# Separate semaphores for the first K halves, with re-made engine orders, in a cosine-similarity attention kernel

## The chip, the cores and the metric

The kernel runs on one NeuronCore of a Trainium2 chip. The metric is the device time of one launch in microseconds (us), as the median of several runs; lower is better. The profile pages and traces used below come from single profiled executions on that core.

## The reference

Q, K and V are f32 arrays of shape 8 x 12 x 512 x 64 (batch, head, sequence, dim), tau is 0.1. Each of the 96 heads is an independent attention over unit-length rows:

```
Q_norm = Q / (norm(Q, axis=-1) + 1e-10)
K_norm = K / (norm(K, axis=-1) + 1e-10)
scores = einsum('bhqd,bhkd->bhqk', Q_norm, K_norm) / tau
weights = exp(scores - max(scores)) ; weights = weights / (sum(weights) + 1e-10)
out = einsum('bhqk,bhkd->bhqd', weights, V)
```

## The kernel before

The 96 heads are worked as 48 pairs, numbered s = 0 to 47. A pair goes through these operations, which the program names by a tuple; this document writes the tuple with dots, so `SQ.3.0` is the tuple ("SQ", 3, 0). The middle number is the pair. For operations with w, w=0 is Q and w=1 is K; h is the head of the pair, c the 128-row chunk of the keys.

- `LD.s.w`: load of Q or K (256 KB, line 289), on the queue of SP. `LV.s`: load of V (256 KB, line 292). Pair 0 is loaded in halves of 128 KB by head, `LD.0.w.h` (line 286), the two Q halves from SP's queue and the two K halves from ACT's.
- `SQ`: squares for the norms. POOL does most of them as one 128x1024 operation per pair (line 313); pair 0 is done in halves (`SQ.0.0.h` on ACT line 227, `SQ.0.1.h` on POOL line 229), and pairs 1 and 2 are split between POOL (line 308) and ACT (line 306).
- `SSQ`: PE adds up the squares into PSUM (line 330). `RED`: DVE finishes the sum (lines 233, 337, 341).
- `LOG`, `NRMS`, `NEW`: the reciprocal root; on ACT by Ln and Exp for pairs 0 to 2 (lines 236, 240, 355, 357), by Newton steps on DVE (lines 362 to 371) for the later groups of two pairs.
- `SCL`: multiply Q or K with it, to bf16 (lines 246 and 389), Q on DVE, K mostly on POOL. `TR`: four transposes on PE (lines 254, 256, 395). `EVA`: copy out of PSUM (lines 265, 267, 402).
- `SCO.s.c`: scores on PE (line 429). `EXP.s.c`: exponential on ACT (line 445), 128x1024 each, four for a pair; the first two chunks of pair 0 are done by head, as `EXP.0.c.h`.
- `VC.s`: V to bf16 on POOL (line 450). `PV`: weights times V on PE (line 459). `RCP`, `NRM`: normalisation on DVE (lines 474, 476). `ST`: store from SP's queue (line 483).

There is no scheduler when the kernel is built: the table `ORDER` lists, for each of the five engines, the numbers of the operations in the sequence in which that engine issues them. The numbers were made ahead of time by a planner, from costs and due times. An engine issues strictly in that sequence; a wait in front of one operation holds back everything behind it, on SP's queue too. Negative numbers in the PE list are filler matmuls of so many columns (line 188), which only keep PE occupied; a `warm` of 8 matmuls of 512 columns (line 185) stands ahead of them and needs the identity matrix that POOL makes (`one`, `eye`; `vone` is a memset of the ones column of V).

Operations that a DMA performs get a semaphore by the name in `slot`; two operations with one name share one semaphore, and each adds 16. The count that a consumer waits for is handed out while the engines are walked in the sequence sp, pool, dve, pe, act:

```
dma_count[o.slot] += 16
o.sem, o.val, o.inc = dma_sems[o.slot], dma_count[o.slot], 16
```

In the kernel before, the halves of pair 0 are called `first{w}_{h}` and the loads of pairs 1 and 2 `first{s}_{w}`. `LD.0.1.0` and `LD.1.0` are thus both `first1_0`, and `LD.0.1.1` and `LD.1.1` both `first1_1`. SP is walked ahead of ACT, so pair 1's load has the value 16 and pair 0's K half the value 32: whoever wants the K half waits for both transfers.

Ring sizes that matter below: 18 buffers of Q and K, 6 of V as loaded (so `LV.s` waits for `VC.(s-6)`), 8 of the output.

Of the kernel before, what the change touches and what calls it, by code (L numbers as in the profile page):

```python
# [106 lines left out]
def bass_cosine_similarity_attention_kernel(  # L107
# [15 lines left out]
    R_QK, R_V, R_SQ, R_QN, R_QT, R_ET, R_O, R_X = 18, 6, 6, 3, 3, 3, 8, 3  # L123
# [27 lines left out]
    P = Program(nc)  # L151
# [10 lines left out]
    group, first = [], []  # L162
# [4 lines left out]
    def src(x, s):  # L167
        b, h = divmod(2 * s, NHEAD)
        return x[b, h : h + 2].rearrange("h (p t) d -> p h (t d)", t=NT)

    def key(name, s, *rest):
        return (name, s) + rest if s >= 0 else None
# [102 lines left out]
    def pair(s):  # L275
# [6 lines left out]
        for w, x in ((0, Q), (1, K)):  # L282
            if s == 0:
                for h in range(2):
                    P.add(("LD", 0, w, h), "act" if w else "sp", "ldh", -1000 + h,  [],
                          lambda e, w=w, x=x, h=h: e.dma_start(out=qk[iq][:, w, h], in_=src(x, s)[:, h]), slot=f"first{w}_{h}")  # L286
                continue
            P.add(("LD", s, w), "sp", "ld", s, [*([("SCL", 0, w, 0), ("SCL", 0, w, 1), ("SQ", 0, w, 0), ("SQ", 0, w, 1)] if s == R_QK else [key("SCL", s - R_QK, w), key("SQ", s - R_QK, w if s - R_QK in SQ_ON else 0)])],
                  lambda e, w=w, x=x: e.dma_start(out=qk[iq][:, w], in_=src(x, s)),
                  slot=f"first{s}_{w}" if s <= 2 else f"qk{iq}")  # L290
# [223 lines left out]
def slack(s, most):  # L514
# [5 lines left out]
        "7 8 64 65 103 104 143 142 187 186 11 297 221 220 66 262 415 263 296 188 264 105 338 339 144 568 63 525 222 372 "  # L520
        "373 416 340 449 796 417 450 298 526 491 492 602 374 493 102 645 644 451 567 797 831 678 527 601 185 754 830 "
        "722 720 141 756 679 950 1059 1103 721 949 261 873 908 219 755 569 646 603 680 1026 984 1060 1213 1289 874 414 "
        "1288 295 907 1178 337 832 1025 371 1255 951 798 1102 983 490 1212 600 448 1366 1136 1407 566 643 1331 1137 524 "
        "1332 909 1365 1061 875 753 1179 1518 1636 677 985 1517 1594 795 1254 1104 719 1027 1408 829 1483 1637 1138 "
        "1670 1180 1595 1333 1214 1441 1256 1290 948 1747 1442 1484 1024 1443 1561 1367 1562 872 1560 1788 906 1712 "
        "1789 982 1409 1519 1596 1746 1713 1101 1671 1485 1672 1058 1748 1177 1135 1822 1824 1287 1253 1823 1364 1440 "
        "1211 1406 1790 1638 1330 1482 1559 1714 1669 1745 1516 1635 1711 1787 1593 1821 1864 1865 "
    ),
    "pool": (
        "0 1 2 4 14 27 22 67 35 107 145 189 50 223 89 265 206 282 128 299 172 341 237 248 271 375 358 418 313 452 347 "  # L530
        "401 494 435 324 424 477 511 528 570 553 466 500 604 647 681 542 576 799 723 587 833 653 757 630 740 664 695 "
        "876 729 952 706 910 771 805 1028 986 782 859 882 816 1105 1062 1139 924 958 1181 893 1215 935 1000 1034 969 "
        "1257 1011 1122 1291 1088 1045 1111 1164 1368 1334 1153 1187 1351 1240 1444 1410 1229 1198 1317 1263 1469 1486 "
        "1393 1563 1340 1546 1520 1274 1427 1597 1382 1416 1622 1715 1673 1458 1492 1503 1580 1639 1774 1851 1569 1791 "
        "1825 1749 1611 1656 1645 1808 1698 1687 1721 1763 1797 1732 1839 "
    ),
    "dve": (
        "5 13 15 26 28 19 32 24 21 72 70 34 75 109 78 76 111 80 114 115 117 147 190 119 149 192 55 150 56 151 152 153 "
        "154 61 155 226 156 157 159 158 62 161 193 163 224 266 100 268 195 227 101 228 94 229 197 230 95 231 139 232 "
        "302 234 233 140 133 235 134 342 239 300 344 183 269 303 184 304 177 305 178 306 273 307 376 308 217 309 310 "  # L540
        "311 211 378 212 218 345 315 419 421 253 379 254 380 453 381 259 382 260 383 349 384 287 455 385 386 288 387 "
        "388 390 422 392 495 497 329 456 293 457 294 458 330 459 426 460 335 461 336 463 462 529 464 363 498 364 531 "
        "369 468 370 571 573 532 406 533 407 534 605 535 412 536 502 537 413 538 440 539 607 441 574 648 540 446 482 "
        "650 447 608 544 609 483 610 682 611 488 612 489 613 578 615 614 616 617 619 516 684 517 522 724 523 621 726 "
        "800 685 558 686 559 687 651 688 564 689 565 690 692 691 655 693 592 598 760 593 599 697 727 758 802 635 761 "
        "636 762 877 763 731 764 641 765 642 766 669 767 768 836 670 769 675 953 676 834 773 803 879 911 837 711 838 "
        "712 839 807 840 717 841 718 842 913 745 844 843 845 846 848 746 751 987 850 752 955 880 914 1029 787 915 788 "
        "916 884 917 793 918 794 919 989 920 921 922 821 956 822 1063 1106 827 926 1031 828 990 864 991 865 992 1140 "
        "993 870 994 871 995 960 996 997 1182 904 998 898 905 899 1065 1002 1032 1216 1108 940 1066 941 1067 946 1068 "
        "1069 947 1070 1258 1071 1036 1072 1073 980 1075 974 1074 981 975 1142 1077 1292 1079 1109 1184 1016 1143 1022 "  # L550
        "1144 1145 1017 1146 1023 1147 1113 1148 1150 1149 1335 1151 1056 1050 1218 1051 1057 1155 1369 1260 1185 1219 "
        "1093 1220 1094 1221 1099 1222 1100 1223 1189 1224 1294 1226 1225 1127 1227 1128 1261 1133 1134 1231 1411 1337 "
        "1445 1295 1169 1296 1170 1297 1265 1298 1175 1299 1487 1300 1203 1371 1301 1176 1302 1204 1303 1304 1306 1209 "
        "1564 1210 1308 1338 1245 1413 1372 1246 1521 1373 1251 1374 1252 1375 1342 1376 1279 1447 1377 1378 1379 1280 "
        "1380 1285 1414 1286 1384 1489 1322 1448 1449 1323 1450 1328 1451 1329 1452 1598 1453 1418 1454 1455 1456 1523 "
        "1674 1356 1357 1716 1362 1460 1490 1398 1566 1363 1524 1399 1525 1526 1527 1528 1529 1530 1494 1404 1531 1405 "
        "1432 1600 1433 1533 1532 1438 1535 1567 1537 1439 1474 1642 1640 1475 1601 1602 1603 1571 1604 1480 1605 1481 "
        "1606 1676 1608 1607 1508 1609 1509 1643 1514 1826 1515 1613 1551 1718 1677 1678 1552 1557 1750 1679 1558 1647 "
        "1680 1681 1682 1752 1585 1683 1586 1684 1792 1591 1685 1592 1689 1794 1753 1719 1754 1755 1627 1756 1628 1757 "
        "1758 1760 1759 1633 1723 1634 1661 1662 1761 1667 1668 1765 1795 1703 1828 1829 1704 1830 1799 1831 1832 1833 "  # L560
        "1709 1834 1710 1737 1835 1836 1837 1743 1738 1744 1841 1785 1786 1779 1780 1813 1814 1819 1820 1856 1857 1862 "
        "1863 "
    ),
    "pe": (
        "6 -512 -256 -256 -256 -192 23 20 -256 -256 71 69 -128 33 36 108 -128 42 38 39 110 79 43 77 46 48 148 146 81 "
        "116 118 83 51 52 53 54 191 85 57 58 87 59 60 225 120 122 160 124 96 97 90 162 126 98 99 164 267 91 166 92 93 "
        "168 194 196 135 136 170 137 138 301 198 129 130 131 132 200 179 180 202 236 238 204 181 173 182 343 240 272 "
        "174 242 175 176 270 244 213 214 246 215 216 207 274 208 209 210 377 276 312 278 314 249 250 280 251 252 420 "
        "255 316 346 256 257 318 283 284 258 348 320 285 286 454 322 289 350 352 290 325 389 354 391 326 327 356 291 "
        "328 496 292 393 425 423 395 331 332 333 334 397 359 399 360 361 365 366 362 427 530 367 368 429 465 467 431 "  # L570
        "402 403 404 433 405 572 501 469 408 409 499 471 410 411 436 437 473 438 439 606 475 442 443 503 444 445 505 "
        "478 479 480 481 649 507 543 541 509 484 485 486 545 487 577 547 575 549 518 519 512 513 514 551 520 515 683 "
        "579 521 618 581 620 554 555 583 556 557 725 585 560 561 622 654 562 624 563 588 589 590 626 652 591 594 595 "
        "628 759 596 597 656 694 696 658 631 637 632 638 660 633 634 801 662 639 640 698 728 730 700 665 666 667 668 "
        "702 835 704 671 672 673 674 732 770 734 707 708 709 772 736 710 713 878 738 806 774 804 714 715 776 716 741 "
        "742 743 778 744 912 780 747 748 749 808 750 847 810 849 783 784 812 785 786 954 814 883 789 851 881 790 853 "
# [64 lines left out]
```

## Time and profile before

| | us |
|---|---|
| median of 9 runs | 194.49 (193.02 to 196.02) |
| time of the profiled execution | 194.47 |
| span in its trace | 192.5 |
| ACT busy (L445 alone) | 182.2 (176.7) |
| PE, DVE, POOL busy | 175.2, 168.4, 155.3 |
| first exponential starts, in the span | 12.19 |

The profiled execution lies on the median of the runs to 0.02 us; 1.97 us of its time are outside the span. The page gives busy time by engine, then by group of instructions with the line of the kernel; the trace behind it gives each engine's instructions in order of time. Times in the text are from the start of the span.

### The profile page before, as it was taken

The page shows a single profiled execution, that of the slowest core. Times are in us where ns is not written, and L with a number is a line of the kernel's source. Part 1 is how long each engine was busy: PE and PEld are TensorE (multiplying, and loading weights), DVE is VectorE, ACT ScalarE, POOL GpSimd, SP SyncE. Part 2 cuts the span into 40 slices and gives each one's busy share as a digit, 9 for nine tenths or more (in the row PEclk, how much of TensorE's full clock was granted, in tenths as well). Part 3 has the DMA queues.
Part 4 walks back from the last instruction along what each step waited for, and adds up shares of the span by engine and source line. Part 5 has one row for each costly group of instructions (what it writes and reads, how often), then busy time and mean ns, then how long its engine had stood idle before and what let it go on. Part 6 is the DMA issues. An engine that isn't in the chain of part 4 may idle for free.

```text
span 192.5 us, 6756 instructions
## 1 busy us (share of the span) xinstructions
PE 175.2 (91%) x2729; PEld 110.6 (57%) x2729; DVE 168.4 (88%) x593; ACT 182.2 (95%) x211; POOL 155.3 (81%) x144
## 2 busy tenths in 40 slices
PE   7399899989999999999899999989899999999993
PEld 2266466646665566566566556656565666555552
DVE  1569999999999999999989999998999999977844
ACT  4469999999999999999999999999999999999993
POOL 2699869999998999999998999897999975524200
PEclk9789999999999999999999999999999999999999
DMA  5999999988999999999299995897692156301067
GB/s 173 356 351 348 296 339 358 361 284 248 348 357 378 337 347 373 379 380 330 100 302 377 363 367 155 251 371 256 217 313 79 56 164 221 110 4 58 0 197 242
DMA packets 52302, 50.76 MB, mean 264 GB/s; under 512 B 3120, under 2 KB 52272, under 8 KB 52272
## 3 DMA queue, kind: packets, MB, share of 16 engines
q1 hardware_dynamic: 51984, 50.08, 79.3%
q8 instruction: 21, 0.34, 0.8%
q10 hardware_dynamic: 288, 0.26, 0.4%
q14 instruction: 9, 0.07, 0.1%
HBM read 37.75 MB, written 12.58 MB: 261 GB/s over the span
## 4 chain that ended last, share of the span: by engine, by line
ACT 82%; DMA 4%; PE 4%; POOL 4%; DVE 2%; issue 1%; SPq 1%; DVEq 0%; POOLq 0%
ACT et L445 81%; DMA out_dram<-ob 2%; DMA qk<-in_Q_dram 2%; POOL sq L313 2%; PE ops L459 1%; DVE ob L476 1%; PE scps L429 1%; POOL vb L450 1%; PE ops L330 1%; POOL qn L389 1%; SPq L286 0%; DVE qn L389 0%; DVE rd L474 0%; PE scps L256 0%; POOL qn L246 0%
## 5 line engine op out<-in xcount | busy, mean ns | idle before, releaser
L445 ACT ACTIVATE et<-scps 128x1024 bf16<-128x1024 f32 (+1 forms) x195 | 176.7, 1169 | 0.3 <-PE scps L429 0.3
L313 POOL TENSOR_TENSOR sq<-qk 128x1024 bf16<-128x1024 f32 x45 | 84.6, 1893 | 1.0 <-DMA qk<-in_Q_dram 0.6
L429 PE MATMUL scps<-qt 64*128 64x512 bf16 x384 | 75.5, 386 | 9.0 <-ACT et L445 4.9
L459 PE MATMUL ops<-vb,et 128*128 128x65 bf16 x1536 | 76.5, 195 | 0.8 <-POOL vb L450 0.5
L459 PEld LDWEIGHTS ops<-vb,et 128*128 128x128 bf16 x1536 | 57.6, 98 | 29.7 <-issue 21.0
L389 POOL TENSOR_TENSOR qn<-qk,rk 128x512 bf16<-128x512 f32 x37 | 38.1, 1042 | 17.1 <-DVE rk L367 16.8
L476 DVE TENSOR_TENSOR ob<-ops,rd 128x256 f32<-128x256 f32 x96 | 39.6, 418 | 1.3 <-DMA out_dram<-ob 0.7
L389 DVE TENSOR_TENSOR qn<-qk,nps 128x512 bf16<-128x512 f32 x57 | 37.8, 677 | 0.0
L429 PEld LDWEIGHTS scps<-qt 64*128 64x128 bf16 x384 | 19.2, 92 | 28.1 <-ACT et L445 11.9
L402 DVE COPY qt<-tps 128x1024 bf16<-128x1024 bf16 x47 | 32.1, 684 | 3.3 <-PE tps L395 2.7
L395 PE MATMUL tps<-ident,qn 128*128 128x128 bf16 x376 | 34.2, 221 | 0.2
L450 POOL TENSOR_SCALAR vb<-vf 128x512 bf16<-128x512 f32 x48 | 29.4, 626 | 4.4 <-DMA vf<-in_V_dram 3.9
L341 DVE TENSOR_REDUCE nps<-sq 128x8 f32<-128x512 bf16 x44 | 29.8, 682 | 0.6 <-POOL sq L313 0.4
L395 PEld LDWEIGHTS tps<-ident,qn 128*128 128x128 bf16 x376 | 21.6, 98 | 11.0 <-issue 5.0
L474 DVE RECIPROCAL rd<-ops 128x4 f32<-128x4 f32 x96 | 16.8, 176 | 6.5 <-PE ops L459 3.8
L330 PE MATMUL ops<-sq,ident 128*128 128x64 bf16 x400 | 20.1, 195 | 0.0
L330 PEld LDWEIGHTS ops<-sq,ident 128*128 128x128 bf16 x400 | 15.3, 99 | 3.1 <-issue 2.5
L337 DVE TENSOR_REDUCE nps<-ops 128x8 f32<-128x64 f32 x46 | 10.1, 219 | 1.8 <-PE ops L330 1.3
L362 DVE TENSOR_TENSOR nps<-nps,ys 128x32 f32<-128x32 f32 (+1 forms) x46 | 8.8, 192 | 0.2
L363 DVE SCALAR_TENSOR_TENSOR nps<-nps,ys 128x32 f32<-128x32 f32 (+1 forms) x46 | 8.8, 191 | 0.3
L233 DVE TENSOR_REDUCE xs<-sq 128x4 f32<-128x256 bf16 x4 | 1.6, 418 | 4.9 <-POOL sq L229 2.5
L367 DVE SCALAR_TENSOR_TENSOR nps<-nps,ys 128x16 f32<-128x16 f32 (+1 forms) x30 | 5.1, 173 | 0.1
(43 smaller groups left out, 39.5 us busy)
## 6 DMA issues: line engine op xcount, KB each, us to landing
vf<-in_V_dram SPq DMA_DIRECT2D x48, 256.0 KB, 6.0
qk<-in_Q_dram SPq DMA_DIRECT2D x47, 256.0 KB, 5.9
qk<-in_K_dram SPq DMA_DIRECT2D x47, 256.0 KB, 5.9
out_dram<-ob SPq DMA_DIRECT2D x47, 256.0 KB, 4.9
qk<-in_Q_dram SPq DMA_DIRECT2D x2, 128.0 KB, 2.5
qk<-in_K_dram ACTq DMA_DIRECT2D x2, 128.0 KB, 2.7
out_dram<-ob SPq DMA_DIRECT2D x2, 128.0 KB, 1.7
```

The lines of the kernel that those rows point to most:

```text
L313: lambda e: e.tensor_tensor(out=sqf, in0=data, in1=data, op=ALU.mult))
L330: last = e.matmul(out=o_ps[bank][:, 320:384], lhsT=ident[:, :], rhs=sq[iqs][:, 8 * w : 8 * w + 8, 8 * k : 8 * k + 8], start=(k == 0), stop ...
L341: lambda e, w=w, dst=dst: e.tensor_reduce(out=dst, in_=sq[iqs][:, 8 * w : 8 * w + 8, :], axis=AX.X, op=ALU.add))
L389: lambda e, w=w, r=r: e.tensor_tensor(out=qn[iqn][:, w].rearrange("p t h d -> p h t d"), in0=qk[iq][:, w].rearrange("p h (t d) -> p h t d" ...
L395: last = e.transpose(t_ps[:, w, t, :], qn[iqn][:, w, t].rearrange("p h d -> p (h d)"), ident[:, :])
L402: lambda e: e.tensor_copy(out=qt[iqt][:, :, :, :].rearrange("p w t x -> p (w t x)"), in_=t_ps[:, :, :, :].rearrange("p w t x -> p (w t x)")))
L429: last = e.matmul(out=sc_ps[:, 2 * b + h, :], lhsT=qt[iqt][64 * h : 64 * h + 64, 1, c, :], rhs=qt[iqt][64 * h : 64 * h + 64, 0, :, :], sta ...
L445: lambda e, c=c, b=b, hs=hs: e.activation(out=et[iet][:, c, hs[0] : hs[-1] + 1, :], in_=sc_ps[:, 2 * b + hs[0] : 2 * b + hs[-1] + 1, :], f ...
L450: lambda e: e.tensor_scalar(out=vb[:, iq, :, :, 0:DIM].rearrange("p c h d -> p h c d"), in0=vf[iv][:, :, :].rearrange("p h (c d) -> p h c ...
L459: last = e.matmul(out=o_ps[h][:, 65 * t : 65 * t + 65], lhsT=et[iet][:, c, h, 128 * t : 128 * t + 128], rhs=vb[:, iq, c, h, :], start=(c = ...
L474: lambda e, h=h, grid=grid: e.reciprocal(out=rd[io][:, h, :], in_=grid[:, :, DIM]))
L476: lambda e, h=h, grid=grid: e.tensor_tensor(out=ob[io][:, h], in0=grid[:, :, 0:DIM], in1=rd[io][:, h, :].unsqueeze(2).to_broadcast([128, N ...
```

## The change

The K halves and the Q halves of pair 0 get names of their own, `head{w}_{h}`, so that no name is shared. The loads of pair 1 get the kind "ld1" in place of "ld"; the kind is a label for the planner and issues nothing. The tables of SP, POOL, DVE and PE are new throughout; that of ACT changes in two places at the head.

```diff
-  ... lambda e, ...: e.dma_start(out=qk[iq][:, w, h], in_=src(x, s)[:, h]), slot=f"first{w}_{h}")
+  ... lambda e, ...: e.dma_start(out=qk[iq][:, w, h], in_=src(x, s)[:, h]), slot=f"head{w}_{h}")
...
-  P.add(("LD", s, w), "sp", "ld", s, ...
+  P.add(("LD", s, w), "sp", "ld1" if s == 1 else "ld", s, ...
...
-        "0 1 2 4 14 27 22 67 35 107 145 189 50 223 89 265 206 282 128 299 172 341 237 248 271 375 358 418 313 452 347 "
+        "4 0 1 2 14 27 22 67 35 107 145 50 189 223 89 128 265 341 299 248 172 206 282 237 324 271 375 418 313 347 452 "
...
-        "6 -512 -256 -256 -256 -192 23 20 -256 -256 71 69 -128 33 36 108 -128 42 38 39 110 79 43 77 46 48 148 146 81 "
+        "6 -256 -256 -256 -256 -256 -256 23 20 -256 -192 69 71 36 33 -128 42 38 108 43 39 110 79 46 77 48 146 148 81 "
...
-        "9 10 3 12 25 16 18 17 29 31 30 68 106 73 74 37 44 40 41 112 45 113 47 49 82 84 86 88 121 123 125 127 165 167 "
+        "9 10 3 12 25 16 18 17 29 31 30 68 106 73 37 74 44 40 41 112 113 45 47 49 82 84 86 88 121 123 125 127 165 167 "
```

Written with names, the stretches that the prediction uses:

```
POOL before  one eye eps vone SQ.0.1.0 SQ.0.1.1 SCL.0.1.0 SQ.1.0 SCL.0.1.1 SQ.2.1 SQ.3 SQ.4 VC.0 SQ.5 VC.1
             SQ.6 VC.4 VC.6 VC.2 SQ.7 VC.3 SQ.8 SCL.5.1 ...
POOL after   vone one eye eps SQ.0.1.0 SQ.0.1.1 SCL.0.1.0 SQ.1.0 SCL.0.1.1 SQ.2.1 SQ.3 VC.0 SQ.4 SQ.5 VC.1
             VC.2 SQ.6 SQ.8 SQ.7 VC.5 VC.3 VC.4 VC.6 SCL.5.1 ...
PE before    warm -512 -256 -256 -256 -192 TR.0.1.0 TR.0.0.0 -256 -256 SSQ.1.1 SSQ.1.0 -128 TR.0.0.1 TR.0.1.1
             SSQ.2.0 -128 SCO.0.1.0 SCO.0.0.0 SCO.0.0.1 SSQ.2.1 TR.1.1 SCO.0.1.1 ...
PE after     warm -256 (six times) TR.0.1.0 TR.0.0.0 -256 -192 SSQ.1.0 SSQ.1.1 TR.0.1.1 TR.0.0.1 -128
             SCO.0.1.0 SCO.0.0.0 SSQ.2.0 SCO.0.1.1 SCO.0.0.1 SSQ.2.1 TR.1.1 SCO.0.2 TR.1.0 SCO.0.3 ...
ACT before   SQ.0.0.0 SQ.0.0.1 LOG.0.0 ... SQ.1.1 SQ.2.0 LOG.1 NEW.1.7 EVA.0.1.1 EXP.0.1.0 ...
ACT after    SQ.0.0.0 SQ.0.0.1 LOG.0.0 ... SQ.1.1 SQ.2.0 LOG.1 EVA.0.1.1 NEW.1.7 EXP.0.1.0 ...
DVE after    ... EVA.0.0.1 NEW.1.6 SCL.1.1 RED.2.0 RED.2.1 SCL.1.0 NEW.2.6 SCL.2.0 EVA.1 SCL.2.1 ...
SP after     the four loads of pair 1 and 2 first, as before; then LD.3.0 LD.3.1 LD.4.0 LV.0 LD.4.1 LD.5.1 LD.5.0 ...
             ... LV.21 LD.26.1 LD.26.0 LV.20 LD.23.0 LD.23.1 LV.23 ST.7 ...
```

## The prediction

> **What bounds the kernel now.** I read the page's busy times first, then the groups, then the first 13 us of the timeline engine by engine.
>
> ```profile
> span 192.5 us, 6756 instructions
> PE 175.2 (91%) x2729; PEld 110.6 (57%) x2729; DVE 168.4 (88%) x593; ACT 182.2 (95%) x211; POOL 155.3 (81%) x144
> ...
> L445 ACT ACTIVATE et<-scps 128x1024 bf16<-128x1024 f32 (+1 forms) x195 | 176.7, 1169 | 0.3 <-PE scps L429 0.3
> ...
> L389 POOL TENSOR_TENSOR qn<-qk,rk 128x512 bf16<-128x512 f32 x37 | 38.1, 1042 | 17.1 <-DVE rk L367 16.8
> ```
>
> ACT bounds it. Its 195 exponentials take 176.7 us and it stood still before them for 0.3 us in total. So the span is three pieces: the time to the first exponential (12.19), an unbroken run on ACT (to 189.2), and a tail (3.3). An earlier start of that run shortens the span one for one, provided the other engines keep up. The second line says how much room they have: POOL idles 17.1 us ahead of its K multiplies, but DVE and PE have little.
>
> The start, on POOL, ACT and PE:
>
> ```profile
> 5.85 1.32 POOL L229 TENSOR_TENSOR sq<-qk 128x256 bf16<-128x256 f32 x2 [3.78 <-DMA qk<-in_Q_dram]
> 7.57 0.61 POOL L246 TENSOR_TENSOR qn<-qk,xs 128x256 bf16<-128x256 f32 x1 [0.39 <-ACT scps L240]
> 8.14 1.04 POOL L308 TENSOR_TENSOR sq<-qk 128x512 bf16<-128x512 f32 x1
> 9.13 0.61 POOL L246 TENSOR_TENSOR qn<-qk,xs 128x256 bf16<-128x256 f32 x1
> 9.71 1.04 POOL L308 TENSOR_TENSOR sq<-qk 128x512 bf16<-128x512 f32 x1
> 10.70 3.74 POOL L313 TENSOR_TENSOR sq<-qk 128x1024 bf16<-128x1024 f32 x2
> ```
>
> ```profile
> 6.95 0.30 ACT L236 ACTIVATE ys<-xs,eps 128x8 f32<-128x8 f32 x1 [2.55 <-DVE xs L233]
> ...
> 10.99 0.31 ACT L355 ACTIVATE ys<-xs,eps 128x16 f32<-128x16 f32 x1 [1.66 <-DVE xs L337]
> 11.33 0.22 ACT L357 ACTIVATE xs<-ys 128x16 f32<-128x16 f32 x1
> 11.57 0.59 ACT L265 ACTIVATE qt<-scps 64x512 bf16<-64x512 bf16 x1
> 12.19 1.57 ACT L445 ACTIVATE et<-scps 128x512 bf16<-128x512 f32 x3
> ```
>
> POOL squares the K halves of pair 0 only at 5.85, released by a load of Q, which these squares don't read: that is the shared semaphore. The issue records, by window, give the landings:
>
> ```profile
> qk<-in_K_dram ACTq DMA_DIRECT2D x1, 128.0 KB, 2.5
> ...
> qk<-in_Q_dram SPq DMA_DIRECT2D x1, 256.0 KB, 4.1
> qk<-in_Q_dram SPq DMA_DIRECT2D x1, 128.0 KB, 2.7
> qk<-in_K_dram ACTq DMA_DIRECT2D x1, 128.0 KB, 3.0
> ```
>
> K halves: issued at 0.79 and 1.24, landed at 3.3 and 4.2. `LD.1.0`: issued 1.69, landed 5.8. By the same view `LD.1.1` lands at 6.5, `LD.2.0` 7.3, `LD.2.1` 8.0, and the later half of pair 3 9.6. The first six loads keep their places on SP's queue, so these stay.
>
> **The start after the change, step by step.**
> - `SQ.0.1.0` at 3.35 to 3.96, `SQ.0.1.1` at 4.25 to 4.9 (0.61 each).
> - DVE (0.42 each): `RED.0.0.0` 3.56 to 3.98, then `RED.0.1.0` to 4.40. `LOG.0.0` starts at 4.42 instead of 6.95, 2.5 us earlier; `SCL.0.1.0` moves from 7.57 to 5.04.
> - Next POOL meets a real landing: `SQ.1.0` waits for 5.8, runs 5.85 to 6.89 (was 8.14); `SCL.0.1.1` 6.89 to 7.5 (was 9.13). ACT's `SQ.1.1` waits for 6.5, ends 7.1; `SQ.2.0` ends 7.9.
> - PE: `SSQ.1.0` and `SSQ.1.1` from 6.93, ready at 7.6. `TR.0.1.1` follows `SCL.0.1.1`: 7.55 to 8.0; `TR.0.0.1` and a filler to 8.3; first `SCO` to 8.7.
> - ACT: `RED.1.1` ends at 7.83, `LOG.1` 7.85 to 8.16, `EVA.0.1.1` 8.17 to 8.76, `NEW.1.7` within it, first exponential **8.9** instead of 12.19: 3.3 us.
> - Pair 0's later chunks: `SQ.2.1` (landing 8.0) ends at 9.07, so `LOG.2` can run by 10.1, before ACT reaches it at 10.4. `EVA.1` on DVE: `SCL.1.0` to 10.65, wait for `NEW.2.7` (10.9), `NEW.2.6`, `SCL.2.0` to 11.7, `EVA.1` to 12.4, `SCO.1.0` to 12.8; ACT wants it at 13.05. No gap.
>
> The exchange of `NEW.1.7` and `EVA.0.1.1` costs nothing: both stand ahead of the first exponential either way. Fillers shrink from 2240 to 2112 columns, on a PE that waits there anyway. The kind "ld1" issues nothing.
>
> **One cost at the head.** `vone` (0.74 us in POOL's timeline) now precedes `one` and `eye`, so PE's warm-up, which needs the identity, starts at 2.15 instead of 1.41. The granted clock in this trace:
>
> ```profile
> 0.83:4.24 3.41, 2.83 (x7) 1.04 (x8) 0.69 (x2) 1.95 (x3) 1.17 (x4) 1.00 0.62 197
> 4.24:7.65 3.41, 1.07 (x7) 0.49 (x5) 1.15 (x4) 0.73 (x4) 1.31 (x3) 1.00 1.02 340
> 7.65:11.06 3.41, 2.83 (x32) 2.53 (x33) 2.06 (x6) 1.71 (x6) 3.41 (x5) 0.50 1.07 360
> ```
>
> Columns: window, length, PE, PEld, DVE, ACT, POOL busy, clock. (Ahead of 4.24 no clock is recorded; the warm matmuls start 0.427 apart there, the 256-column fillers after it 0.11, so the clock was half and was released at 4.24.) After the stretch with PE busy for only 1.07 of 3.41 us the clock is 0.50 for the next one; the K transposes and sums of pairs 0 and 1 fall in it. After the change PE waits from about 5.5 to 5.7, not 5.3 to 8.2, so by this row the halving goes. [...]
>
> **Does the rest keep up?** The operations and their durations are the same; only places change.
> - POOL. Its chain of full-size squares starts at 10.70 now, and at 9.65 after (landing of pair 3): only 1.05 us earlier. Up to `SCL.5.1` stand 6 squares (1.87, from 3.74 for two), 7 V casts (0.60 start to start) and one multiply (1.0): 16.4, so `SCL.5.1` ends at 26.1. It ended at 28.43, held from 25.95 by DVE's norms (idle 1.45 at L389), which now come 3 us sooner. Then transpose 0.45 and `EVA.5` 0.7: 27.25. ACT's pace puts `SCO.5.0` at 30.27 - 3.3 = 27.0. **Late by 0.3.** The same count for `SCL.7.1` gives 32.4 against 32.5 wanted by the transposes, and for `SCL.17.1` 69.0, `EVA.17` 70.5 against 71.0. No other K multiply comes within 1 us.
> - DVE. Work ahead of `EVA.3`, start to start, is 9.5 us in both orders; it ended at 22.8, so 13.3 idle before it. After: `EVA.1` at 12.4 with 3.1 of work is 9.3 idle, about 10 by `EVA.3` after the norms of pair 4: 19.5, wanted at 22.92 - 3.3 = 19.6.
> - ACT's own small waits in a new order: between 0 and the 2.4 us that would be left of POOL's former idle time; nearest row 0.3 (L445). I take 0.3.
> - SP: stores and loads mixed anew. `SPq` waits are covered by the 18 buffers; price below.
>
> **Sum.** 3.3 - 0.3 (POOL at pair 5) - 0.3 = 2.7. The profiled time is 194.47, on the median (194.49): **191.8 us.** The tail is taken as it is: last stores and `NRM.47` follow the last exponential in the same order.
>
> **The rivals.**
> [...]
> - *POOL carries only its own 1.05 us*: if POOL can't give up its former idle time, ACT starts early and then waits at pairs 5 to 17, and 1.05 is all that is left: 193.4. For: POOL is busy 20.0 of 20 us from 40 to 60. Against: that count has to lose 2 us at `SCL.5.1`, where the trace shows POOL standing.
> - *SP and POOL in a circle, slower*: `LV.20` waits for `VC.14` on POOL (about 62.0), and `LD.23.0`, `LD.23.1` stand behind it on SP, issued at about 62.6 and 63.1. `SQ.23` is due on POOL at 69.9, and loads take 5.9 us or more to land: under 1 us of room. If the room is missed by a whole turn (POOL waits for the load, the next V load waits for POOL), one landing of 5.9 less 0.7 of slack at `SCL.19.1` goes to ACT: 191.8 + 5.2 = 197.0. It is slower than before once ACT loses over 2.7 us. For: SP waits 27.1 us for `vb` already. Against: those waits cost ACT nothing now.
> - *The semaphore wasn't what held*: 194.5. Against: 3.78 us of POOL idle, released by a Q load.
>
> **How the numbers follow.** The measurement can tell about 0.5% (1 us). Chances: forecast 0.47, cold clock 0.22, POOL's 1.05 0.17 (half of it within 1 us of before), circle 0.10, no effect 0.04. Faster 0.78, same 0.12, slower 0.10. Low end: 3.3 with no loss gives 191.2, less 0.4 for the spread of medians, 190.8. High end 194.4 takes in all but the circle. The forecast's own range is 190.8 to 192.4.
>
> **What would show it.** Right: `SQ.0.1.0` near 3.4 with no Q load as releaser, first exponential at 8.7 to 9.1, clock 1.00 from 4.2 on, ACT idle at L445 under 1 us, most of it near `SCO.5.0`. Wrong: a clock of 0.50 within 5 to 8 us; POOL idle on DMA at L313 past 60 us; ACT idle over 2 us at L445.

## The result, and the profile after

The changed kernel takes 192.23 us (median of 17 runs, 191.51 to 193.77). The kernel before was run beside it and has 195.48 over all of its 54 runs. The ratio is 0.9877, 95% interval 0.9855 to 0.9899: faster by 1.2%, about 2.4 us. (The ratio leaves out runs more than 1.5% above the fastest of their kernel, which is why it is nearer to 1 than the two medians, 3.2 us apart, are.) The forecast was 2.7 us.

The profiled execution took 192.08 us, with a span of 190.3 against 192.5. The page's first lines and the groups of ACT's exponentials, POOL's squares and POOL's K multiplies:

```profile
span 190.3 us, 6755 instructions
...
PE 173.9 (91%) x2729; PEld 110.1 (58%) x2729; DVE 169.6 (89%) x593; ACT 182.6 (96%) x211; POOL 155.3 (82%) x144
...
L445 ACT ACTIVATE et<-scps 128x1024 bf16<-128x1024 f32 (+1 forms) x195 | 176.6, 1125 | 0.3 <-PE scps L429 0.3
L313 POOL TENSOR_TENSOR sq<-qk 128x1024 bf16<-128x1024 f32 x45 | 84.8, 1893 | 6.3 <-DVE qt L402 3.8
...
L389 POOL TENSOR_TENSOR qn<-qk,rk 128x512 bf16<-128x512 f32 x37 | 38.3, 1042 | 8.3 <-DVE rk L367 6.4
```

ACT does the same work (176.6 us of exponentials) with the same 0.3 us of idle time. So all of the difference lies ahead of the run of exponentials. POOL's idle time before its K multiplies fell from 17.1 to 8.3 us, but that before its squares rose from 1.0 to 6.3: a part of the room has been used, and the larger part has only moved to another place in POOL's list. POOL and ACT at the start, from the timeline:

```profile
3.76 1.18 POOL L229 TENSOR_TENSOR sq<-qk 128x256 bf16<-128x256 f32 x2 [1.73 <-DMA qk<-in_K_dram]
5.47 0.61 POOL L246 TENSOR_TENSOR qn<-qk,xs 128x256 bf16<-128x256 f32 x1 [0.53 <-ACT scps L240]
6.54 1.04 POOL L308 TENSOR_TENSOR sq<-qk 128x512 bf16<-128x512 f32 x1 [0.45 <-DMA qk<-in_Q_dram]
7.53 0.61 POOL L246 TENSOR_TENSOR qn<-qk,xs 128x256 bf16<-128x256 f32 x1
8.68 1.04 POOL L308 TENSOR_TENSOR sq<-qk 128x512 bf16<-128x512 f32 x1 [0.53 <-DMA qk<-in_K_dram]
10.18 1.89 POOL L313 TENSOR_TENSOR sq<-qk 128x1024 bf16<-128x1024 f32 x1 [0.46 <-DMA qk<-in_K_dram]
```

```profile
7.20 1.35 ACT L306 ACTIVATE sq<-qk 128x512 bf16<-128x512 f32 x2 [1.08 <-DMA qk<-in_K_dram]
8.59 0.31 ACT L355 ACTIVATE ys<-xs,eps 128x16 f32<-128x16 f32 x1
8.92 0.59 ACT L265 ACTIVATE qt<-scps 64x512 bf16<-64x512 bf16 x1
9.53 0.21 ACT L357 ACTIVATE xs<-ys 128x16 f32<-128x16 f32 x1
9.77 1.57 ACT L445 ACTIVATE et<-scps 128x512 bf16<-128x512 f32 x3
```

The releaser of the K squares is now a load of K, at 3.76 instead of 5.85. The squares at 6.54, 8.68 and 10.18 name a load too, where before only the first did: POOL's squares now follow the landings. The first exponential starts at 9.77 instead of 12.19, 2.4 us earlier. Following single operations through both traces, this lead is 2.25 us at `EXP.1.0`, 2.19 at `EXP.5.0`, 2.02 at `EXP.20.0` and 2.21 at `EXP.47.0`: what was won at the start is carried through, and neither grows nor is eaten.

### The profile page after: what moved, and what is told of

It reads as the page before. It is cut to its first block, busy times and chain, and to the rows that moved or that the text cites. A ratio compares the mean times of both kernels' runs of the same rounds, so it can differ in the third digit from the quotient of the medians.

```text
span 190.3 us, 6755 instructions
## 1 busy us (share of the span) xinstructions
PE 173.9 (91%) x2729; PEld 110.1 (58%) x2729; DVE 169.6 (89%) x593; ACT 182.6 (96%) x211; POOL 155.3 (82%) x144
## 4 chain that ended last, share of the span: by engine, by line
ACT 84%; PE 5%; POOL 3%; DMA 3%; DVE 2%; issue 1%; SPq 0%; ACTq 0%; POOLq 0%
ACT et L445 84%; DMA qk<-in_Q_dram 3%; PE scps L429 2%; PE ops L459 1%; POOL sq L313 1%; DVE ob L476 1%; PE tps L395 1%; DVE qt L402 1%; PE ops L330 1%; POOL vb L450 1%; POOL sq L308 1%; POOL qn L389 1%; SPq L286 0%; DVE nps L341 0%; DVE qn L389 0%
## 5 line engine op out<-in xcount | busy, mean ns | idle before, releaser
L445 ACT ACTIVATE et<-scps 128x1024 bf16<-128x1024 f32 (+1 forms) x195 | 176.6, 1125 | 0.3 <-PE scps L429 0.3
L459 PE MATMUL ops<-vb,et 128*128 128x65 bf16 x1536 | 78.3, 195 | 0.8 <-ACT et L445 0.8
L459 PEld LDWEIGHTS ops<-vb,et 128*128 128x128 bf16 x1536 | 58.6, 98 | 29.7 <-issue 20.6
L395 PE MATMUL tps<-ident,qn 128*128 128x128 bf16 x376 | 35.2, 221 | 1.3 <-POOL qn L389 0.8
L395 PEld LDWEIGHTS tps<-ident,qn 128*128 128x128 bf16 x376 | 21.6, 98 | 12.5 <-issue 5.4
L330 PEld LDWEIGHTS ops<-sq,ident 128*128 128x128 bf16 x400 | 14.8, 98 | 4.1 <-issue 2.7
L185 PE MATMUL ops<-warm_in,ident 128*128 128x512 bf16 x8 | 3.5, 621 | 2.0 <-POOL eps L178 2.0
```

The costliest lines, as they stand in the source:

```text
L330: last = e.matmul(out=o_ps[bank][:, 320:384], lhsT=ident[:, :], rhs=sq[iqs][:, 8 * w : 8 * w + 8, 8 * k : 8 * k + 8], start=(k == 0), stop ...
L395: last = e.transpose(t_ps[:, w, t, :], qn[iqn][:, w, t].rearrange("p h d -> p (h d)"), ident[:, :])
L445: lambda e, c=c, b=b, hs=hs: e.activation(out=et[iet][:, c, hs[0] : hs[-1] + 1, :], in_=sc_ps[:, 2 * b + hs[0] : 2 * b + hs[-1] + 1, :], f ...
L459: last = e.matmul(out=o_ps[h][:, 65 * t : 65 * t + 65], lhsT=et[iet][:, c, h, 128 * t : 128 * t + 128], rhs=vb[:, iq, c, h, :], start=(c = ...
```

## The experiments

The theory is that the shared semaphore held the start, and that the tables only have to keep up with an earlier one. The rivals are: the tables carry the gain; the gain is PE's clock; POOL can't follow.

**Semaphores alone.** This is the kernel before with its own tables:

```diff
-  ... slot=f"first{w}_{h}")
+  ... slot=f"head{w}_{h}")
```

> The kernel before with only the names of pair 0's semaphores changed (head in place of first), its own old tables kept. Theory 1 (the shared semaphore held the start, the tables only keep up): POOL's first square of K starts near 3.5 instead of 5.85, the first exponential 2 to 2.6 us earlier than 12.19, and the time falls by 1.5 to 2.6 us, ACT idle at L445 stays under 1 us. Theory 2 (the old tables can't follow an earlier start, the new ones carry the gain): first exponential earlier, but ACT idles over 1 us more at L445 and the time falls by less than 1 us.

It took 192.8 us (4 runs), ratio 0.9881, interval 0.9815 to 0.9947 (ratios are to the kernel before). POOL and ACT:

```profile
3.45 0.61 POOL L229 TENSOR_TENSOR sq<-qk 128x256 bf16<-128x256 f32 x1 [1.38 <-DMA qk<-in_K_dram]
...
9.79 1.57 ACT L445 ACTIVATE et<-scps 128x512 bf16<-128x512 f32 x3
```

This is the same start as the changed kernel's, from one changed string. In this profile the ACT idle time at L445 was 0.2 us.

**Tables alone.** This is the changed kernel with the shared names:

```diff
-  ... slot=f"head{w}_{h}")
+  ... slot=f"first{w}_{h}")
```

> The changed kernel with the old, shared semaphore names, so only the new tables. Theory 1 (semaphore): squares of K at 5.8 to 6.5 as before, first exponential at 11.5 to 12.5, time within 1 us of before. Theory 2 (tables): time falls by over 1 us without the semaphores.

It took 195.08 us (10 runs), ratio 1.0005, interval 0.9951 to 1.0058: nothing, to within 1.1 us.

```profile
6.13 0.61 POOL L229 TENSOR_TENSOR sq<-qk 128x256 bf16<-128x256 f32 x1 [4.10 <-DMA qk<-in_Q_dram]
...
12.40 1.57 ACT L445 ACTIVATE et<-scps 128x512 bf16<-128x512 f32 x3
```

The Q load is the releaser again and the start is where it was. The two runs settle that the semaphore held the start; whether the tables help once the start is early is asked below.

**One half alone.** This is the kernel before with a semaphore of its own for the first K half only:

```diff
-  ... slot=f"first{w}_{h}")
+  ... slot=f"head{w}_{h}" if (w, h) == (1, 0) else f"first{w}_{h}")
```

> The kernel before with a semaphore of its own for the first K half alone (LD.0.1.0); the second (LD.0.1.1) still shares with LD.1.1; old tables. Theory 1 (POOL takes its work in turn, so either shared semaphore alone holds the start): SQ.0.1.0 near 3.5, but SQ.0.1.1 waits for LD.1.1 until 6.4 to 7.2 and SCL.0.1.0 stands behind it at 7.0 to 7.8; first exponential at 11.5 to 12.4, time within 0.6 us of before. Theory 2 (each half is worth its share): first exponential about 1.2 us earlier, time down by 1.0 to 1.4 us.

It took 194.58 us (12 runs), ratio 1.0005, interval 0.9971 to 1.0039: nothing, to within 0.8 us. POOL:

```profile
3.67 0.61 POOL L229 TENSOR_TENSOR sq<-qk 128x256 bf16<-128x256 f32 x1 [1.60 <-DMA qk<-in_K_dram]
6.26 0.61 POOL L229 TENSOR_TENSOR sq<-qk 128x256 bf16<-128x256 f32 x1 [1.98 <-DMA qk<-in_K_dram]
6.83 0.61 POOL L246 TENSOR_TENSOR qn<-qk,xs 128x256 bf16<-128x256 f32 x1
```

The first square runs early, and then POOL stands 1.98 us ahead of the second, whose semaphore pair 1's K load still shares. The multiply that pair 0 needs is queued behind it, so the second false wait still holds it after the first has gone. The first exponential of this profile is at 10.71, and that is a miss for the first theory, which had 11.5 to 12.4. The second load had landed at 6.2, and no halved clock followed; nine of the twelve runs had a mean clock of 0.986 to 0.991 against 0.999 here, so this profile isn't typical. Over the runs no gain shows.

**The clock.** This is the kernel before with 22 more fillers ahead of its first transpose, so that PE works where it waited:

```diff
-        "6 -512 -256 -256 -256 -192 23 20 ...
+        "6 -512 -256 -256 -256 -192 -256 (22 times) 23 20 ...
```

> The kernel before with 22 more fillers of 256 columns (0.11 us each at full clock, 2.4 us) ahead of its first transpose, so that PE is busy where it waited from 5.3 to 8.2; semaphores and tables otherwise as before. Theory 1 (part of the gain is the clock): no window at 0.50 after 7.65, the transposes and sums of pairs 0 and 1 take half the time, first exponential 0.5 to 1.0 us earlier than 12.19, time down by 0.4 to 1.0 us. Theory 2 (the wait for the squares alone): clock 1.00, but the first exponential and the time move by less than 0.3 us.

It took 194.31 us (10 runs), ratio 1.0003, interval 0.9965 to 1.0042. The window that had the clock at 0.50 in the kernel before:

```profile
7.65:11.06 3.41, 3.38 (x54) 2.62 (x52) 2.68 (x9) 2.21 (x8) 3.41 (x6) 1.00 1.09 367
```

Its clock is 1.00, and this one profile has its first exponential at 11.62, 0.57 earlier than before, as expected, and it still has that lead at pair 47. The ratio shows none of it, but its interval leaves room for 0.7 us. The clock is therefore not what gave 2.4 us; that it gives some tenths is neither shown nor excluded.

The mean clocks of the single runs say how often this matters. In the kernel before, 52 of the 62 runs that stood beside these experiments had 0.991 or less. The stretch of 3.41 us at half clock in the profile before (7.65 to 11.06) takes 0.009 off the mean clock of its span of 192.5 us, so each of these runs lost at least as much. Of the 24 runs of the changed kernel one had as little, and of the 16 with the semaphores alone also one. The median time of the kernel before is 193.8 us over its 10 runs with a mean clock above 0.995, 194.7 over the 38 with 0.986 to 0.991, and 196.1 over the 14 with 0.978 to 0.983. So with the early start most of this time at half clock is gone, and each 0.009 went with about 1 us. How much of that 1 us is the clock's own doing is open: nine of the ten filled runs also had over 0.995, and their median is 194.2; so had six of the ten with the tables alone, which gained nothing.

**The identity first on POOL.** This is the changed kernel with the order of the kernel before for four small operations:

```diff
-        "4 0 1 2 14 27 ...
+        "0 1 2 4 14 27 ...
```

> The changed kernel with POOL making the identity first, as in the kernel before (one eye eps vone). Theory 1 (PE's clock is released before the transposes either way): PE's warm-up starts at 1.4 instead of 2.04, first exponential within 0.3 us of the changed kernel's 9.77, time within 0.4 us of the changed kernel. Theory 2 (the late warm-up costs a window of the clock in part of the executions): the time falls by 0.5 us or more below the changed kernel, and its runs spread less.

It took 192.16 us (4 runs), ratio 0.9848, interval 0.9784 to 0.9912. PE's warm-up started at 1.41, and the first exponential at 10.00, later than with the late warm-up. This kernel, the changed kernel and the semaphores alone were then run again, side by side on one chip:

> The changed kernel once more, beside the next two on one chip. Ratio to before 0.985 to 0.990; first exponential between 9.2 and 9.9, by when LD.1.0 lands (5.8 to 6.6).

> Only the semaphores changed, old tables, beside the changed kernel. Theory 1 (the tables add nothing by themselves): within 0.5 us of the changed kernel. Theory 2 (the new tables carry part of the gain): over 0.8 us above the changed kernel.

> The changed kernel with the identity first on POOL, beside the changed kernel. Theory 1 (the late warm-up costs nothing): within 0.4 us of the changed kernel. Theory 2 (it costs part of the executions a window of half clock): 0.5 us or more below the changed kernel.

| kernel | median us (runs) | ratio to before | first exponential | ACT idle at L445 |
|---|---|---|---|---|
| changed kernel | 192.11 (6) | 0.9889 [0.9855, 0.9923] | 9.53 | 0.5 |
| semaphores alone | 193.10 (12) | 0.9913 [0.9874, 0.9952] | 9.56 | 1.3 |
| identity first | 192.17 (9) | 0.9887 [0.985, 0.9924] | 9.79 | 0.7 |

The late warm-up costs nothing that these runs can tell: 192.17 against 192.11. The tables are the open point. The medians of old and new differ by 1.0 us, beyond what the first theory allowed. Ten of the twelve runs with the old tables lie above the longest of the changed kernel's six (192.30), but the kernel with the identity first, which has the new tables too, reached 193.09 and once 195.94, and the intervals overlap widely.

One part of it shows in the profiles, at the head. From the start of `SQ.1.1` to the first exponential it took 2.82 us in both profiles with old tables and free landings, and 2.58 to 2.61 in the five with new ones (listed below). With the old tables, `LOG.1` waits for the second of pair 1's two sums on DVE, which PE adds up in the other order there. This is ACT in the first run with the semaphores alone:

```profile
8.59 0.31 ACT L355 ACTIVATE ys<-xs,eps 128x16 f32<-128x16 f32 x1 [0.33 <-DVE xs L337]
```

With the new tables it doesn't wait for DVE. That is worth 0.24 us, which the prediction didn't count. Later the old tables can lose time too; ACT with them in the repeat, 67 to 73 us:

```profile
67.28 3.08 ACT L445 ACTIVATE et<-scps 128x1024 bf16<-128x1024 f32 x3
70.81 1.02 ACT L445 ACTIVATE et<-scps 128x1024 bf16<-128x1024 f32 x1 [0.45 <-PE scps L429]
72.11 1.02 ACT L445 ACTIVATE et<-scps 128x1024 bf16<-128x1024 f32 x1 [0.28 <-PE scps L429]
```

ACT waits at pair 16 (0.45 and 0.28) and at pair 4 (0.50). The PE row just ahead names the cause there: transposes that wait 0.61 us for a K multiply on POOL.

```profile
70.05 0.40 PE L395 MATMUL tps<-ident,qn 128*128 128x128 bf16 x4 [0.61 <-POOL qn L389]
```

In the repeat of the changed kernel nothing stands at pair 16, but ACT waits 0.19 and 0.25 us at pair 4. And in the first run with the semaphores alone ACT's idle time was only 0.2. So beyond the 0.24 us at the head, whether the new tables are worth anything is not settled; by the medians they are worth up to 1 us in all.

**POOL's room at pair 5.** This is the changed kernel with one square moved ahead of the K multiply:

```diff
-  pool: ... VC.6 SCL.5.1 VC.7 SCL.6.1 SQ.9.0 SQ.10.0 ...
+  pool: ... VC.6 SQ.9.0 SCL.5.1 VC.7 SCL.6.1 SQ.10.0 ...
```

> The changed kernel with SQ.9.0 (1.87 us on POOL) moved from behind SCL.5.1, VC.7 and SCL.6.1 to just ahead of SCL.5.1; nothing else. Theory 1 (POOL has the room at pair 5 that the traces show: EVA.5 ended 0.2 us before SCO.5.0 started): SCL.5.1 ends 1.9 us later, ACT idles 1.5 to 1.8 us more at L445 near 28 us, and that time isn't made good later: time 1.4 to 1.8 us above the changed kernel. Theory 2 (POOL has more room than the count gives, the forecast lateness at pair 5 was a phantom): time within 0.6 us of the changed kernel.

It took 194.95 us (10 runs), ratio 0.9983, interval 0.995 to 1.0016. Against 0.9877 that is 1.1% or about 2.1 us, somewhat more than the first theory's 1.4 to 1.8: nearly the whole gain is gone. The profile shows where; it caught the longest of the ten executions (196.57), so its lines are read for the place, not for the size. PE, and then the windows (window, length, busy time of PE, PEld, DVE, ACT and POOL, clock, DMA share, GB/s):

```profile
29.02 0.61 PE L395 MATMUL tps<-ident,qn 128*128 128x128 bf16 x4 [2.31 <-POOL qn L389]
```

```profile
27.40:30.80 3.40, 1.78 (x18) 1.12 (x18) 1.14 (x2) 0.87 (x2) 3.40 (x5) 0.69 1.07 350
30.80:34.20 3.40, 3.40 (x29) 1.77 (x26) 2.90 (x13) 2.48 (x3) 1.61 (x1) 0.50 1.08 367
```

The transposes of pair 5 stand in PE's list ahead of `SCO.4.3`, so PE itself stood for 2.31 us, and ACT with it. During that wait, at 28.7, the clock fell to 0.50, and then PE, busy without a gap, was too slow to feed ACT, which was busy for only 2.48 of 3.40 us. The other runs bear this out. The four with a mean clock of 0.997 or more took 193.65 to 194.25 us, about 2 us above the changed kernel, near the 1.87 us that the square takes. The five with 0.990 or 0.991, as 3.41 us at half clock make it, took 194.9 to 195.49. One late multiply was thus paid twice in most runs.

**Pair 0 ahead of pair 1's sums.** This is the changed kernel with the head reordered:

```diff
-  act:  SQ.1.1 SQ.2.0 LOG.1 EVA.0.1.1 NEW.1.7 EXP.0.1.0 EXP.0.0.0 EXP.0.0.1 LOG.2 NEW.2.7 ...
+  act:  SQ.1.1 EVA.0.1.1 SQ.2.0 EXP.0.1.0 LOG.1 NEW.1.7 EXP.0.0.0 EXP.0.0.1 LOG.2 NEW.2.7 ...
-  pe:   -192 SSQ.1.0 SSQ.1.1 TR.0.1.1 TR.0.0.1 -128 SCO.0.1.0 SCO.0.0.0 SSQ.2.0 SCO.0.1.1 SCO.0.0.1 ...
+  pe:   -192 TR.0.1.1 TR.0.0.1 -128 SCO.0.1.0 SCO.0.0.0 SSQ.1.0 SSQ.1.1 SCO.0.1.1 SCO.0.0.1 SSQ.2.0 ...
-  pool: SQ.1.0 SCL.0.1.1   ...  VC.6 SCL.5.1
+  pool: SCL.0.1.1 SQ.1.0   ...  SCL.5.1 VC.6
-  dve:  RED.1.0 RED.1.1 EVA.0.0.1
+  dve:  EVA.0.0.1 RED.1.0 RED.1.1
```

> The changed kernel with the head reordered so that pair 0's first exponentials no longer stand behind pair 1's sums: POOL SCL.0.1.1 ahead of SQ.1.0 and SCL.5.1 ahead of VC.6; PE the transposes and first scores of pair 0 ahead of SSQ.1; ACT SQ.1.1 EVA.0.1.1 SQ.2.0 EXP.0.1.0 LOG.1 NEW.1.7 EXP.0.0.0 and so on; DVE EVA.0.0.1 ahead of RED.1.0. Theory 1 (the start is now held by pair 1's landing through LOG.1, which ACT reaches ahead of the exponentials): first exponential at 8.6 to 9.1, but the same work stands on ACT until pair 1, so only its 0.4 to 0.6 us of idle time are won: 0.3 to 0.6 us below the changed kernel. Theory 2 (DVE and POOL set the pace up to pair 5): the first exponential is earlier and ACT then waits the same time at pairs 1 to 5: within 0.2 us of the changed kernel.

It took 193.04 us (6 runs), ratio 0.9912, interval 0.9878 to 0.9946: not better than the changed kernel, a miss for the first theory, and 0.7 us worse by the ratios, a miss for the second too. The first exponential came at 9.35, but then:

```profile
9.85 0.30 ACT L355 ACTIVATE ys<-xs,eps 128x16 f32<-128x16 f32 x1
...
11.62 0.31 ACT L355 ACTIVATE ys<-xs,eps 128x16 f32<-128x16 f32 x1 [0.26 <-DVE xs L337]
...
14.88 1.02 ACT L445 ACTIVATE et<-scps 128x1024 bf16<-128x1024 f32 x1 [0.39 <-PE scps L429]
```

`LOG.1`, which all of pair 1 needs, had moved from 8.59 to 9.85. Pair 1's exponentials started at 14.88 instead of 13.97, with ACT idle ahead of them. In this profile PE also had half clock from 12.5 to 15.9 (0.71 on average from 11.06 to 14.47), so the 0.9 us may not be the order's alone.

**The same with pair 1's K square on DVE:**

```diff
-SQ_ON = {1: ("pool", "act"), ...
+SQ_ON = {1: ("pool", "dve"), ...
-  act:  SQ.1.1 EVA.0.1.1 ...        dve:  EVA.0.0.0 EVA.0.0.1 ...
+  act:  EVA.0.1.1 ...               dve:  EVA.0.0.0 SQ.1.1 EVA.0.0.1 ...
```

> As the kernel with the reordered head, and SQ.1.1 (0.6 us on ACT) moved to DVE, which waits there from 7.3 to 8.1. Theory 1 (ACT's work ahead of pair 1 is what counts): another 0.4 to 0.6 us, 0.7 to 1.1 us below the changed kernel in all. Theory 2 (DVE and POOL set the pace up to pair 5): within 0.3 us of the changed kernel, with ACT idle at L445 over 0.5 us.

It took 192.06 us (6 runs), ratio 0.987, interval 0.9834 to 0.9906: the changed kernel's ratio, although ACT has 0.6 us less to do ahead of pair 1. The idle time at L445 was 0.3 us, not over 0.5, so the first theory has missed, and the second has the time right and the place wrong. ACT stood still elsewhere:

```profile
7.91 0.59 ACT L265 ACTIVATE qt<-scps 64x512 bf16<-64x512 bf16 x1 [1.98 <-PE scps L254]
```

It waited 1.98 us for a transpose ahead of `EVA.0.1.1`, and 0.26 ahead of `LOG.2`, which follows pair 2's landing. Up to pair 1 its idle time was 3.3 us against the changed kernel's 2.5: the work that was taken off ACT became waiting. Pair 1's exponentials began at 14.21, near the changed kernel's 13.97. No version tried beats the changed kernel by more than the noise.

**Holding back the loads behind pair 1.** In the changed kernel `LD.2.0` now waits for the first square of K:

```diff
-  P.add(("LD", s, w), "sp", ..., s, [*(...
+  P.add(("LD", s, w), "sp", ..., s, [*([("SQ", 0, 1, 0)] if (s, w) == (2, 0) else []), *(...
```

> The changed kernel with LD.2.0, and all loads behind it on SP's queue, held back until POOL has squared the first K half (about 4.4 instead of 2.7). Theory 1 (the loads behind share the DMA engines with pair 1's and delay their landing): LD.1.0 lands 0.4 us or more earlier than 6.5, LOG.1 and the first exponential as much earlier; the loads of pairs 2 and 3 land 1 to 1.7 us later and hold POOL at SQ.2.1 and SQ.3.0, so the time is 0.5 to 1.7 us above the changed kernel. Theory 2 (transfers are served in turn): LD.1.0 lands at 5.8 to 6.8 as in the other profiles, first exponential at 9.5 to 10.1, and the time is 1.0 to 1.7 us above the changed kernel for the later pairs alone.

It took 192.78 us (4 runs), ratio 0.9891, interval 0.985 to 0.9931. `LD.1.0` took 4.3 us to land; in the other thirteen profiles it took 3.8 to 5.0. One profile inside that spread can't tell whether the loads behind delay it; both theories had allowed for its landing at 5.95. The first exponential was late (10.46), because `SQ.2.0` stands ahead of `LOG.1` on ACT and now waited for its load:

```profile
8.75 0.63 ACT L306 ACTIVATE sq<-qk 128x512 bf16<-128x512 f32 x1 [1.50 <-DMA qk<-in_Q_dram]
```

Of the expected loss, at least 0.5 us by either theory, the ratios show 0.3, and their intervals reach from none to 1.1.

## Why the prediction was right, point by point

- **What held the start.** Right in the releaser, the place and the chain, as the two runs that part semaphores and tables show.
- **K squares at 3.35.** They started at 3.76: the half landed after 2.9 us instead of 2.5.
- **First exponential at 8.9.** It was 9.77; this term was mis-sized most, by 0.87. Of this 0.7 is the landing of pair 1: `LD.1.0` took 4.8 us here instead of 4.1, and `LD.1.1` 5.0 instead of 4.3.

```profile
qk<-in_Q_dram SPq DMA_DIRECT2D x1, 256.0 KB, 4.8
qk<-in_K_dram SPq DMA_DIRECT2D x1, 256.0 KB, 5.0
```

  The prediction carried the landings of one execution over. They differ between executions, and this start follows them: in the five profiles that have the new tables and free landings, `SQ.1.1` starts as soon as `LD.1.1` has landed, and the first exponential follows 2.58 to 2.61 us later.

| profile | SQ.1.1 starts | first exponential |
|---|---|---|
| square ahead of SCL.5.1 | 6.63 | 9.21 |
| changed kernel again | 6.95 | 9.53 |
| changed kernel | 7.20 | 9.77 |
| identity first, again | 7.21 | 9.79 |
| identity first | 7.39 | 10.00 |

  The sum had 2.4 for this stretch. The other 0.2 is `NEW.1.7`, which was put within `EVA.0.1.1`; it ran behind it (9.53, 0.21 us), as the kernel before's rows at 11.33 and 11.57 already have the two in turn. The sum also let pair 1's sums alone hold `LOG.1`. In all five profiles `LOG.1` starts less than 0.1 us after `SQ.2.0` has ended on ACT, so the load of Q for pair 2 holds the start as much as pair 1's loads do.
- **No gap in pair 0.** Nearly: 2.41 at the first exponential became 2.25 at `EXP.1.0`. `LOG.2` and `NEW.2.7` now stand one behind the other on ACT, which leaves 0.34 us between exponentials ahead of `EXP.0.1.1`; the kernel before had 0.07 there and 0.10 ahead of `EXP.0.2`.
- **POOL late by 0.3 at pair 5.** The count held: from the first full-size square to the end of `SCL.5.1` it took 16.5 us where 16.4 was counted. `SCL.5.1` ended at 26.64 (26.1 was worked out), `EVA.5` at 27.82. Since the start was 0.9 later than worked out, this was 0.2 in time for `SCO.5.0` at 28.05 and not late. In the repeat of the changed kernel ACT does wait at pair 4:

```profile
25.09 2.85 ACT L445 ACTIVATE et<-scps 128x1024 bf16<-128x1024 f32 x3 [0.19 <-PE scps L429]
28.20 1.94 ACT L445 ACTIVATE et<-scps 128x1024 bf16<-128x1024 f32 x2 [0.25 <-PE scps L429]
```

  The 0.25 us stands one score earlier than the wait was placed: the transposes of pair 5 stand ahead of `SCO.4.3` in PE's list. But it isn't the count that brought it. POOL started its squares 0.2 us earlier than in the first profile, and then stood 1.05 us ahead of `SQ.8.0` for a load of Q:

```profile
20.28 3.75 POOL L313 TENSOR_TENSOR sq<-qk 128x1024 bf16<-128x1024 f32 x2 [1.05 <-DMA qk<-in_Q_dram]
```

  `SCL.5.1` ended at 27.38, 17.4 us after the first square. The load, `LD.8.0`, was issued at 11.93 and landed at 20.21; in the first profile it was issued at 12.07 and landed at 19.13. The prediction put such waits at nothing ("covered by the 18 buffers"). The run with the square ahead shows that there is no more room.
- **DVE at pair 3.** Right: 0.1 us to spare was worked out, and `EVA.3` ended at 20.57 for `SCO.3.0` at 20.71, both later by the late start.
- **ACT's own small waits, 0.3.** It was 0.3 at L445, in one place, ahead of `EXP.33.2`.
- **Cold clock.** Not what happened: no run shows the loss that was given 0.22 of the chances. In the profile after the clock was released at 5.34, 1.1 us later than the 4.2 given for it, and stayed at 1.00 up to 189.7. Pair 1's sums ran in it: 16 matmuls in 0.66 us, where the kernel before took 1.06 us for them at 0.50.
- **SP and POOL in a circle.** Its first half is there. `LD.23.1` was issued at 66.3, not 63.1, and POOL waited for it:

```profile
71.49 3.74 POOL L313 TENSOR_TENSOR sq<-qk 128x1024 bf16<-128x1024 f32 x2 [0.46 <-DMA qk<-in_K_dram]
```

  It cost 0.46 us on POOL, not a whole landing, and `EVA.19` was still 1.7 us ahead of its score.
- **Sum.** 3.3 - 0.3 - 0.3 was worked out. It was 2.4 at the start, less 0.2 by pair 47; the parts were off by 0.9 and 0.4 in opposite directions, and 2.7 came near to 2.4 partly for that reason, which is luck. The measured 192.2 lies inside the forecast's own range, 190.8 to 192.4.

## What to carry to other kernels

When an engine's first wait names a transfer that its operand doesn't come from, look for a semaphore with two owners: changing one string was worth 0.9 to 1.2% here, and freeing only one of two such waits in a row brought nothing that twelve runs could show. Count how much work a slower engine has ahead of the consumer in either order, from start-to-start times; here that count (16.4 us) was right to 0.1, but it says nothing of a load that lands late in between. And take a landing from several executions before a sum rests on it.

## What the runs showed of the hardware that was not expected

- **The clock's first release came 6 us apart for the same start of PE.** PE started at 2.04 both in the profile after and in that of the tables alone. The clock was released at 5.34 in the one and at 11.38 in the other. These are the three stretches up to the release with the tables alone (columns as in the windows of the square ahead). No clock is recorded ahead of the release, and the rows then print 1.00; but the six 256-column fillers that start at 5.43 take 1.49 us, and those that start at 5.39 in the profile after 0.82.

```profile
1.14:4.55 3.41, 2.51 (x6) 0.88 (x7) 0.46 (x2) 2.12 (x3) 0.82 (x4) 1.00 0.64 202
4.55:7.97 3.42, 2.37 (x9) 1.06 (x7) 0.79 (x3) 0.57 (x3) 1.30 (x3) 1.00 0.99 307
7.97:11.38 3.41, 2.86 (x33) 2.62 (x34) 2.23 (x7) 1.81 (x6) 3.41 (x5) 1.00 1.07 359
```

  In other profiles the release came at 4.24 (the kernel before), 4.79 (the square ahead), 6.94 (one half alone, with PE busy for 2.70 of the 3.41 us ahead of it) and 7.24 (the identity first, again). From the release on, the clock held each value for 3.41, 3.41 and 180.9 us in the kernel before, and for 184.3 us in the profile after: 1, 1, 53 and 54 times 3.413. What sets the moment of the release isn't shown.
- **A stall of PE was paid twice**: with the square ahead PE waited 2.31 us, up to 29.02, and the clock was at 0.50 for 6.8 us from 28.7 on; in the kernel before it waited 2.92 us, up to 8.23, and the clock was at 0.50 for 3.41 us from 7.65 on.
- **A first load's landing varies by over 1 us** from one execution to the next: 3.8 to 5.0 us for `LD.1.0`, always issued at 1.7.
